# Two-way gated DeltaNet scan on one core: the block inverses of two neighbouring latent tiles in one eight-head group, decays worked in the loaded tile, one ring of six for a step's loads

## The chip, the cores and the metric

The kernel runs on one core of a Trainium2 chip. The metric is the device time of one execution in microseconds. Before the change three runs gave 2559.43, 2563.19 and 2557.81 us, a median of 2559.43.

## What is computed

One step of a diffusion backbone with one layer: 128 context rows and 2048 latent rows of width 1024. Adaptive RMSNorm, one input projection, then two groups of heads side by side (a bidirectional gated DeltaNet with 4 heads of 128, and a gMLP), one output projection, a gated residual, and a squared-ReLU MLP with its own residual. The part that the change touches is the DeltaNet in chunks of 128 rows:

```
a_mat = where(strict, (k_beta @ k.T) * decay, 0)          # per chunk and head, 128 x 128
sol   = triangular_solve(a_mat + I, [v*beta, k_beta*exp(g)])
qk    = (q @ k.T) * decay
v_new = u - w @ S;   o = qd @ S + qk @ v_new;   S = S*exp(g_last) + kd.T @ v_new
```

`decay[i, j]` is exp(g_i - g_j) for j up to i and 0 beyond, where g is the running sum of the log gates. The chunks of one direction form a chain through the state S. The backward direction is the same on the flipped sequence. The inverse of (a_mat + I) does not depend on S, so it can be made ahead of the chain.

## The kernel before

**Stages.** The trace shows three. Up to about 440 us the input projection, the convolution and the first projections of the gMLP run. From about 440 to 1205 us runs the scan. From 1205 us to the end run the MLP's products with weights and activations split into a high and a low part (three matmuls each, L241, L242 and L243, of 128 x 512).

**Units.** A tile is 128 rows of one sequence: one context tile and 16 latent ones. A unit is one tile in one direction, all four heads. There are 34: units 0 to 16 go forward, 17 to 33 backward, and 0 and 17 are the context tile. The turn from forward to backward lies at about 868 to 892 us. While the units run, TensorE fills the room between their steps with large projections, the "fills": gate, u and v projections of the gMLP in the forward half, the output projection in the backward half.

**The preparation of a unit** (called prep, 15 steps) makes T, the inverse times beta/2:

1. Decay E (L1054 Abs of g_j - g_i per head, L1055 Exp, both on ScalarE). The rows of g lie in tile gb, loaded as one row repeated on all partitions (L990). GpSimd then makes a strict triangle Es (L1059) and an inclusive one E (L1061).
2. KK, the loaded k k^T (L1031), is multiplied by beta and Es (L1071, VectorE, one instruction a head), GpSimd sets its diagonal to one (L1075), ScalarE casts it to f16 as AH (L1080), and VectorE cuts X, the 2 x 2 diagonal blocks, from it (L1081).
3. Y is X transposed: a matmul with the identity (L1089) and a ScalarE cast (L1091). VectorE makes AL = KK - AH (L1092).
4. For each block size s of 2, 4, 8, 16 and 32 two steps. The **A step**: four 128 x 64 matmuls AH by Y (L1109), then VectorE multiplies the product in PSUM by a mask into P (L1113). The **B step**: four matmuls X by P (L1122) and four P by X (L1124), then ScalarE casts the results into Y (L1125) and X (L1126). So each A step needs the Y cast of the level below, and each B step needs the P of its own A step.
5. Level 64 in two steps (L1141 to L1153), one refinement R (L1159 to L1162, VectorE), and T (L1171, ScalarE, one instruction a head).

After level 2's B step VectorE also multiplies the loaded QK = q k^T by E (L1129).

**The scan of a unit** is four steps of four 128 x 128 f32 matmuls each (helper L1026): S,kT into vt (L1183), and S,qT into o; vt,T into vs and vn (L1196, L1198, the latter on ScalarE); vs,kt into the new S (L1212); vn,QK into the output o (L1226 to L1233).

**Loads.** All DMAs are issued by SyncE in the order of the program. An issue waits until its destination is free, and what stands behind it waits too. gb, kt, kT, vt and qT have two buffers each, QK has three, and E, Es and KK share a ring of six. A QK load waits for the vn,QK matmuls of three units before.

**Order.** Each step is emitted at an event time (`at`, in units of a tile; WINDOWS holds starts and ends), a fill's first matmul is held behind the latest chain or prep matmul (LAG2 and LAG3 say which), and a scheduler with its own timeline then fixes the order on each engine. `calm` holds an operation behind the newest level operations. On the chip every engine takes its instructions in that written order.

Of the kernel before, what the change touches and what calls it, by code (L numbers as in the profile page):

```python
# [8 lines left out]
F32 = mybir.dt.float32  # L9
# [8 lines left out]
P = 128  # L18
# [3 lines left out]
NT = 17  # L22
# [8 lines left out]
def interleave(*lists):  # L31
# [5 lines left out]
    for _, _, _, s in sorted(order, key=lambda e: e[:3]):  # L37
# [4 lines left out]
BA = 3  # L42
BX = 3
BT = 1
NS = 4
NE = 6
AHEAD_OF = {0: (("v", 7), ("u", 0)), 1: (("u", 1), ("u", 2)), 2: (("u", 3), ("u", 4))}
# [12 lines left out]
WINDOWS = [2.46, 0.03, -0.51, 1.06, -1.61, 18.16, 17.58, 18.3,  # L60
           2.63, -0.06, -0.18, 1.0, 1.36, 1.64, 1.66, 2.66, 3.17, 3.71]
# [3 lines left out]
def hybrid_step(  # L65
# [82 lines left out]
    def bc4(ap):  # L148
        return ap.unsqueeze(1).to_broadcast([P, 4, P])
# [810 lines left out]
    with ExitStack() as ph:  # L960
# [17 lines left out]
        def f16(tag, bufs=1):  # L978
            return pp.tile([P, 4, P], F16, tag=tag, name=tag, bufs=bufs)
# [4 lines left out]
        def s32(name):  # L984
            return pp.tile([P, 4, P], F32, tag="e", name=name, bufs=NE)

        def load_rows(src, t, d):
            gb = q32("gb", 2)
            rows = src[t * 8 + d * 4 : t * 8 + d * 4 + 4, :].rearrange("a b -> (a b)").unsqueeze(0)
            load(out=gb.rearrange("p h d -> p (h d)"), in_=rows.to_broadcast([P, 512]))  # L990
            return gb

        identq = f16("identq")
        V.tensor_copy(identq, bc4(ident16))
# [21 lines left out]
        def unit(t, d):  # L1016
# [7 lines left out]
            def quad(p, lhs, rhs):  # L1024
                for h in range(H):
                    T.matmul(p[:, h, :], lhs[:, h, :], rhs[:, h, :], start=True, stop=True)  # L1026

            def prep_loads():
                u["gb"] = load_rows(g_d, t, d)
                u["KK"] = s32("KK")  # L1030
                load(out=u["KK"], in_=kk_d[t])  # L1031

            def qk_load():
                u["QK"] = q32("QK", 3)
                load(out=u["QK"], in_=qk_d[t])

            def scan_loads():
                for nm, src in (("kt", kt_d), ("kT", kT_d), ("vt", vt_d), ("qT", qT_d)):
                    u[nm] = q32(nm, 2)
                    if nm in ("kT", "qT"):  # L1040
                        load(out=u[nm], in_=src[t])
                    else:
                        load(out=u[nm], in_=src[t * P : (t + 1) * P, :].rearrange("p (h d) -> p h d", h=H))

            prep = []
            scan = []

            @prep.append
            def _():
                e = s32("E")  # L1050

                def decay():
                    for h in range(H):
                        A.activation(e[:, h, :], u["gb"][:, h, :], AF.Abs, scale=-1.0, bias=col(gcol, h))  # L1054
                    A.activation(e, e, AF.Exp, scale=-1.0)  # L1055

                calm(decay, 2)
                es = s32("Es")
                G.affine_select(out=es, in_=e, pattern=[[0, 4], [-sg, P]], compare_op=ALU.is_gt, fill=0.0,  # L1059
                                base=0, channel_multiplier=sg)  # L1060
                G.affine_select(out=e, in_=e, pattern=[[0, 4], [sg, P]], compare_op=ALU.is_ge, fill=0.0,  # L1061
                                base=0, channel_multiplier=-sg)
                u["Es"], u["E"] = es, e

            @prep.append
            def _():
                a = u["KK"]

                def decayed():
                    for h in range(H):  # L1070
                        V.scalar_tensor_tensor(out=a[:, h, :], in0=a[:, h, :], scalar=col(beta, h),  # L1071
                                               in1=u["Es"][:, h, :], op0=ALU.mult, op1=ALU.mult)

                calm(decayed, 1 if d else 2)
                G.affine_select(out=a, in_=a, pattern=[[0, 4], [1, P]], compare_op=ALU.not_equal, fill=1.0,  # L1075
                                base=0, channel_multiplier=-1)
                u["AH"], u["AL"], u["X"] = f16("AH", BA), f16("AL", BA), f16("X", BX)

                def parts():
                    A.copy(u["AH"], a)  # L1080
                    V.tensor_tensor(out=u["X"], in0=u["AH"], in1=bc4(bd2), op=ALU.mult)  # L1081

                calm(parts)

            @prep.append
            def _():
                p = pd()
                for h in range(H):
                    T.matmul(p[:, h, :], u["X"][:, h, :], ident16, start=True, stop=True)  # L1089
                u["Y"] = f16("Y", BX)  # L1090
                A.copy(u["Y"], p)  # L1091
                V.tensor_tensor(out=u["AL"], in0=u["KK"], in1=u["AH"], op=ALU.subtract)  # L1092

            def level(s):

                def half(ap, i):
                    return ap.rearrange("p h (a t b) -> p h a t b", t=2, b=s)[:, :, :, i, :]

                def packed(p, i):
                    return p[:, :, i * 64 : i * 64 + 64].rearrange("p h (a b) -> p h a b", b=s)  # L1100

                yi = 1 - d

                @prep.append
                def _():
                    p = pd()
                    pp, y = packed(p, 0), half(u["Y"], yi)
                    for h in range(H):
                        T.matmul(pp[:, h], u["AH"][:, h, :], y[:, h], start=True, stop=True)  # L1109
                    u["P"] = pms[s]  # L1110
                    if t == 0:
                        V.tensor_copy(pms[s], identq)
                    V.tensor_tensor(out=half(u["P"], yi), in0=pp, in1=half(bc4(sm[s]), yi), op=ALU.mult)  # L1113
                    level_done(s)

                @prep.append
                def _():
                    p = pd()
                    py, px = packed(p, 0), packed(p, 1)
                    y, x, pm = half(u["Y"], yi), half(u["X"], 1 - yi), half(u["P"], yi)  # L1120
                    for h in range(H):
                        T.matmul(py[:, h], u["X"][:, h, :], pm[:, h], start=True, stop=True)  # L1122
                    for h in range(H):
                        T.matmul(px[:, h], u["P"][:, h, :], x[:, h], start=True, stop=True)  # L1124
                    A.copy(y, py)  # L1125
                    A.copy(x, px)  # L1126
                    level_done(s)
                    if s == 2:
                        V.tensor_tensor(out=u["QK"], in0=u["QK"], in1=u["E"], op=ALU.mult)  # L1129

            for s in (2, 4, 8, 16, 32):
                level(s)

            lo, hi = slice(0, 64), slice(64, P)
            ra, rb = (lo, hi) if d == 0 else (hi, lo)

            @prep.append
            def _():
                p = pd()
                for h in range(H):  # L1140
                    T.matmul(p[:, h, 0:64], u["AH"][:, h, :], u["Y"][:, h, rb], start=True, stop=True)  # L1141
                A.activation(pms[64][ra, :, rb], p[ra, :, 0:64], AF.Copy, scale=-1.0)

            @prep.append
            def _():
                p = pd()
                for h in range(H):
                    T.matmul(p[:, h, 0:64], u["X"][:, h, :], pms[64][:, h, rb], start=True, stop=True)
                for h in range(H):
                    T.matmul(p[:, h, 64:P], pms[64][:, h, :], u["X"][:, h, ra], start=True, stop=True)  # L1150
                V.tensor_copy(u["Y"][ra, :, rb], p[ra, :, 0:64])
                level_done(64)
                A.copy(u["X"][rb, :, ra], p[rb, :, 64:P])  # L1153

            @prep.append
            def _():
                p = pd()
                for h in range(H):
                    T.matmul(p[:, h, :], u["AH"][:, h, :], u["Y"][:, h, :], start=True, stop=False)  # L1159
                    T.matmul(p[:, h, :], u["AL"][:, h, :], u["Y"][:, h, :], start=False, stop=True)  # L1160
                u["R"] = f16("R", 1)
                V.scalar_tensor_tensor(out=u["R"], in0=p, scalar=-1.0, in1=bc4(two16), op0=ALU.mult,  # L1162
                                       op1=ALU.add)

            @prep.append
            def _():
                p = pd()
                quad(p, u["X"], u["R"])
                u["T"] = q32("T", BT)
                for h in range(H):  # L1170
                    A.activation(u["T"][:, h, :], p[:, h, :], AF.Copy, scale=col(hbeta, h))  # L1171
# [940 lines left out]
```

## Time and profile before

| what | us |
|---|---|
| runs: median (lowest to highest) | 2559.43 (2557.81 to 2563.19) |
| span of the profiled execution, first to last instruction | 2557.2 |
| forward units, 440 to 868 | 428.0, of it TensorE busy 426.5 |
| turn, 868 to 892 | 24.0, of it TensorE busy 21.0 |
| backward units, 892 to 1205 | 313.0, of it TensorE busy 308.2 |
| VectorE, ScalarE, GpSimd busy in the whole span | 1826.9, 1259.7, 227.5 |

The profiled execution's span lies 2.2 us below the median of the runs; what surrounds the span is no part of it.

A row of a timeline gives the start, the duration, the engine, the line, the operation with out<-in, and in brackets the idle time of the engine just before it and what ended it. A group gives count, total busy time, mean duration in ns, then the engine's idle time before these instructions and what ended most of it. PE is TensorE, PEld its weight loads, DVE VectorE, ACT ScalarE, POOL GpSimd, SPq the DMA queue of SyncE.

### The profile page before, as it was taken

The numbers are of one execution on the slowest core, as the hardware profiler recorded it, in microseconds if no ns is written. First come the engines' busy times: TensorE is split into PE (matmuls) and PEld (weight loads), VectorE is DVE, ScalarE is ACT, GpSimd is POOL, SyncE is SP. The second block draws the span as 40 slices with busy tenths as digits, with TensorE's granted clock in tenths as the row PEclk, the third lists the DMA queues.
The fourth block names the chain that finished last, engine by engine and source line by source line (L and its number), as shares of the span: only waits on it lengthen the run. The fifth ranks groups of instructions, "written<-read, shape, count | busy, mean of one in ns | idle before, by whom it ended". The sixth has DMA issues, their size and how long they took to land.

```text
span 2557.2 us, 44375 instructions
## 1 busy us (share of the span) xinstructions
PE 2532.0 (99%) x15268; PEld 2133.5 (83%) x15268; DVE 1826.9 (71%) x3790; ACT 1259.7 (49%) x3119; POOL 227.5 (9%) x448
## 2 busy tenths in 40 slices
PE   9999999999999999999999999999999999999998
PEld 5899999788888788888888888888887888888887
DVE  5867746777677878886677877777665557684875
ACT  4755555555555767763455544444442433243442
POOL 3112212111111111110000000000000000000000
PEclk9999999999999999999999999999999999999999
DMA  8977747754445657885877789655489979786673
GB/s 286 303 227 208 211 117 230 246 165 154 146 157 166 217 186 247 270 294 181 300 221 232 245 289 338 198 174 176 143 268 365 336 269 329 249 263 208 223 261 112
DMA packets 503912, 588.66 MB, mean 230 GB/s; under 512 B 36148, under 2 KB 298588, under 8 KB 500102
## 3 DMA queue, kind: packets, MB, share of 16 engines
q1 hardware_dynamic: 503686, 585.82, 70.6%
q8 instruction: 120, 1.97, 0.3%
q14 instruction: 106, 0.87, 0.1%
HBM read 406.01 MB, written 179.67 MB: 229 GB/s over the span
## 4 chain that ended last, share of the span: by engine, by line
PE 86%; DMA 7%; DVE 3%; ACT 2%; issue 1%; SPq 0%; POOL 0%; POOLq 0%; DVEq 0%; ACTq 0%
PE f L241 16%; PE f L243 16%; PE f L242 16%; PE pj L241 7%; PE pj L242 7%; PE pj L243 7%; PE pd L1026 5%; PE pm L241 2%; PE pm L243 2%; PE pm L242 2%; DMA r<-in_w_ff_dram 1%; PE pt L625 1%; DMA raw<-in_w_mod_dram 1%; PE pt L584 1%; PE pd L1109 1%
## 5 line engine op out<-in xcount | busy, mean ns | idle before, releaser
L241 PE MATMUL f<-hop,zH 128*128 128x512 f32 (+1 forms) x976 | 376.4, 386 | 1.8 <-ACT zH L1572 1.8
L243 PE MATMUL f<-hop,zL 128*128 128x512 f32 (+1 forms) x976 | 376.4, 386 | 0.0
L242 PE MATMUL f<-hop,zH 128*128 128x512 f32 (+1 forms) x976 | 376.2, 386 | 0.0
L241 PE MATMUL f<-hop,wH 128*128 128x512 f32 x896 | 349.6, 391 | 1.4 <-ACT p L1645 0.8
L242 PE MATMUL f<-hop,wH 128*128 128x512 f32 x896 | 348.7, 389 | 0.0
L243 PE MATMUL f<-hop,wL 128*128 128x512 f32 x896 | 347.5, 389 | 0.0
L1572 ACT CAST zH<-zraw 128x512 fp32r<-128x512 f32 x240 | 147.0, 620 | 307.8 <-DVE zraw L1566 84.6
L241 PEld LDWEIGHTS f<-hop,zH 128*128 128x128 f32 x976 | 183.3, 188 | 39.8 <-ACT zH L1572 3.3
L243 PEld LDWEIGHTS f<-hop,zL 128*128 128x128 f32 x976 | 183.3, 188 | 38.4 <-DVE zL L1566 1.7
L242 PEld LDWEIGHTS f<-hop,zH 128*128 128x128 f32 x976 | 183.3, 188 | 37.0 <-issue 0.2
L1566 DVE TENSOR_TENSOR zL<-zraw,zH 128x512 fp32r<-128x512 f32 x240 | 162.9, 687 | 61.7 <-ACT zH L1572 49.9
L241 PEld LDWEIGHTS f<-hop,wH 128*128 128x128 f32 x896 | 168.2, 188 | 37.1 <-ACT p L1645 2.0
L243 PEld LDWEIGHTS f<-hop,wL 128*128 128x128 f32 x896 | 168.2, 188 | 35.4
L242 PEld LDWEIGHTS f<-hop,wH 128*128 128x128 f32 x896 | 168.2, 188 | 34.5
L241 PE MATMUL pj<-kH,wH 128*128 128x386 f32 (+2 forms) x568 | 190.5, 338 | 1.7 <-ACT junk L601 1.1
L243 PE MATMUL pj<-kH,wL 128*128 128x386 f32 (+2 forms) x568 | 189.7, 335 | 0.0
L242 PE MATMUL pj<-kL,wH 128*128 128x386 f32 (+2 forms) x568 | 189.4, 335 | 0.0
L184 POOL TENSOR_TENSOR r<-rsq,nhalf 128x1 f32<-128x1 f32 (+1 forms) x37 | 23.8, 643 | 1381.3 <-DVE rsq L183 1381.3
L571 DVE SCALAR_TENSOR_TENSOR cv<-pj,vec,cv 128x384 f32<-128x384 f32 (+2 forms) x164 | 87.0, 539 | 53.6 <-ACT cv L568 52.2
L1572 ACT CAST wH<-s 128x512 fp32r<-128x512 f32 x96 | 59.4, 621 | 124.5 <-DVE s L1566 112.4
L202 DVE TENSOR_TENSOR wL<-raw,wH 128x512 fp32r<-128x512 f32 x120 | 81.4, 684 | 42.2 <-ACT wH L201 38.1
L241 PEld LDWEIGHTS pj<-kH,wH 128*128 128x128 f32 x568 | 107.0, 189 | 5.3 <-issue 2.6
(423 smaller groups left out, 5782.6 us busy)
## 6 DMA issues: line engine op xcount, KB each, us to landing
zraw<-z_d SPq DMA_DIRECT2D x212, 256.0 KB
raw<-in_w_ff_dram SPq DMA_DIRECT2D x192, 256.0 KB
hop<-hop_d SPq DMA_DIRECT2D x28, 1024.0 KB
z_d<-c SPq DMA_DIRECT2D x96, 256.0 KB
zraw<-s_d SPq DMA_DIRECT2D x96, 256.0 KB
raw<-in_w_mod_dram SPq DMA_DIRECT2D x80, 256.0 KB
r<-in_w_ff_dram SPq DMA_DIRECT2D x80, 256.0 KB
s_d<-s SPq DMA_DIRECT2D x64, 256.0 KB
```

The source lines that it names most:

```text
L184: G.tensor_tensor(out=out, in0=t[:np_, :n], in1=nhalf[:np_, :n], op=ALU.pow)
L202: V.tensor_tensor(out=lo, in0=raw, in1=f32(h), op=ALU.subtract)
L241: T.matmul(ps, lh, rh, start=first and i == 0, stop=False, skip_group_check=more)
L242: T.matmul(ps, lh, rl, start=False, stop=False, skip_group_check=more)
L243: T.matmul(ps, ll, rh, start=False, stop=last and i == n - 1, skip_group_check=more)
L571: V.scalar_tensor_tensor(out=cv[:, o : o + m], in0=ps[:, s + sh : s + sh + m], scalar=convw[:, w, j : j + 1], in1=cv[:, o : o + m], op0=AL ...
L584: T.transpose(pq[:, i * P : (i + 1) * P], u["x2"][:, i * P : (i + 1) * P], ident)
L625: T.matmul(ps[:, i * P : (i + 1) * P], kTt[:, i * P : (i + 1) * P], rhs[:, i * P : (i + 1) * P], start=True, stop=True)
L1026: T.matmul(p[:, h, :], lhs[:, h, :], rhs[:, h, :], start=True, stop=True)
L1109: T.matmul(pp[:, h], u["AH"][:, h, :], y[:, h], start=True, stop=True)
L1566: V.tensor_tensor(out=out, in0=a, in1=b, op=op)
L1572: A.copy(h, src)
```

## The change

Two neighbouring units of a direction now form a **group** (units 0 and 17 stay alone; 1-2, 3-4 and so on, 18 groups in all). A group's prep has the same 15 steps, each on eight heads in tiles of 128 x 8 x 128:

- One VectorE or ScalarE instruction does for both tiles what two did: P (now L1202), the casts Y and X (L1213, L1214), AH, X, AL, the level-64 pieces and Exp. Still one a tile or a head: Abs (L1138), KK (L1149), the casts of the first Y (L1174), R and T. The matmuls are the same ones in the same number.
- g is loaded straight into E (L1125), which has one buffer; Es is gone. KK (L1126) has one buffer. Both triangles are selected on KK and on E in place. Abs and Exp work in place on E. E is read last when VectorE multiplies the second tile's QK by it (L1130), which is emitted after the B step of level 16; for the first tile it stays after level 2.
- kT, vt, qT and kt of a step (L1030, L1032) share one ring of six buffers.
- AH, X and Y have two buffers, T two. A group's prep is spread over 2.2 (forward) or 2.3 (backward) tile times, where a unit's was spread over 2.46 or 2.63; the group is emitted at its first unit's time. The loads of QK come at i - 2.6 or i - 2 where they came at i - 3, the loads of E and KK at i - 2.7.

```
 def f16(tag, bufs=1):
-    return pp.tile([P, 4, P], F16, tag=tag, name=tag, bufs=bufs)
+    return pp.tile([P, 2 * H, P], F16, tag=tag, name=tag, bufs=bufs)
 def s32(name):
-    return pp.tile([P, 4, P], F32, tag="e", name=name, bufs=NE)
+    return pp.tile([P, 2 * H, P], F32, tag=name, name=name, bufs=1)
...
+        def prep_loads():
+            g["E"], g["KK"] = s32("E")[:, :nh], s32("KK")[:, :nh]
+            for i, u in enumerate(us):
...
+                load(out=g["E"][:, heads(i)].rearrange("p h d -> p (h d)"), in_=rows.to_broadcast([P, 512]))
+                load(out=g["KK"][:, heads(i)], in_=kk_d[t])
+        def decayed_qk(i):
+            u = us[i]
+            V.tensor_tensor(out=u["QK"], in0=u["QK"], in1=g["E"][:, heads(i)], op=ALU.mult)
...
+                for h in range(nh):
+                    T.matmul(pp[:, h], g["AH"][:, h, :], y[:, h], start=True, stop=True)
...
+                V.tensor_tensor(out=half(pm, yi), in0=pp, in1=half(bch(sm[s], nh), yi), op=ALU.mult)
...
+                A.copy(y, py)
+                A.copy(x, px)
+                level_done(s)
+                if s == 2:
+                    decayed_qk(0)
+                elif s == 16 and n == 2:
+                    decayed_qk(1)
...
-WINDOWS = [2.46, 0.03, -0.51, 1.06, -1.61, 18.16, 17.58, 18.3,
-           2.63, -0.06, -0.18, 1.0, 1.36, 1.64, 1.66, 2.66, 3.17, 3.71]
+WINDOWS = [2.2, 0.03, -0.51, 1.06, -1.61, 18.16, 17.58, 18.3,
+           2.3, -0.06, -0.18, 1.0, 1.36, 1.64, 1.66, 2.66, 3.17, 3.71]
```

**Where the order moves.** Three places, in the forward half. The first is TensorE just ahead of a B step of level 2 before the change. Rows are of unit 5: P_5790 is the P of level 2, P_5793 that of level 16 of unit 4, L241 to L243 are fills:

```order
L1124 MATMUL pd<-X,P_5793 128x64
L1124 LDWEIGHTS P_5793
L1124 MATMUL pd<-X,P_5793 128x64
L1026 MATMUL pd<-vt,T 128x128 x4
L241 MATMUL pm<-wH,hH 128x512
L242 MATMUL pm<-wL,hH 128x512
L243 MATMUL pm<-wH,hL 128x512
L241 MATMUL pm<-wH,hH 128x512
L242 MATMUL pm<-wL,hH 128x512
L243 MATMUL pm<-wH,hL 128x512
L1122 LDWEIGHTS X
L1122 MATMUL pd<-P_5790,X 128x64
```

Its A step stands further up, ahead of the other unit's level. After the change, the same place of the group of units 7 and 8, with P_5788 as the P of level 2:

```order
L241 MATMUL pj<-wL,hH 128x512
L242 MATMUL pj<-wH,hL 128x512
L1199 LDWEIGHTS AH
L1199 MATMUL pd<-Y,AH 128x64
L1199 LDWEIGHTS AH
L1199 MATMUL pd<-Y,AH 128x64
L1199 LDWEIGHTS AH
L1199 MATMUL pd<-Y,AH 128x64
L1199 LDWEIGHTS AH
L1199 MATMUL pd<-Y,AH 128x64
L1210 LDWEIGHTS X
L1210 MATMUL pd<-P_5788,X 128x64
```

The second four matmuls of the A step (the first four stand six fills higher) are followed at once by the B step that reads P_5788. The second place is SyncE's queue. Before, the loads of g went into gb and waited for ScalarE (its Abs on that buffer, two units earlier):

```order
L1035 DMA QK_8428<-qk_d_68 128x512 [waits DMAHW3_49,PE_49]
L1235 DMA of_d_70<-o_8321 128x512 [waits DMAHW4_49,DVE_49]
L1290 DMA gate_d_71<-gw_8749 128x512 [waits DMAHW5_49,DVE_49]
L1043 DMA vt_9049<-vt_d_66 128x512 [waits DMAHW6_49,PE_49]
L990 DMA gb_9374<-g_d_69 128x512 [waits DMAHW7_49,Activation_49]
L1031 DMA KK_9055<-kk_d_67 128x512 [waits DMAHW0_49,Pool_49]
L1043 DMA kt_9045<-kt_d_65 128x512 [waits DMAHW1_49,PE_49]
```

After, they go into E and wait for VectorE, whose last reader of E is the multiplication of QK_8885, loaded two rows higher behind a wait for TensorE:

```order
L1301 DMA hL_8955<-hL_d_62 128x512 [waits DMAHW4_49,PE_49]
L1024 DMA QK_8885<-qk_d_68 128x512 [waits DMAHW5_49,PE_49]
L1098 DMA of_d_70<-o_8504 128x512 [waits DMAHW6_49,DVE_49,Activation_49]
L1125 DMA E_8975<-g_d_69 128x512 [waits DMAHW7_49,DVE_49]
L1125 DMA E_8975<-g_d_69 128x512 [waits DMAHW0_49]
```

The third place is ScalarE. Before, the Abs of a unit stand between a Y and X cast of one level and the next without a wait of their own:

```order
L1125 CAST Y<-pd 128x128x2 [waits PE_49,Activation_49]
L1126 CAST X<-pd 128x128x2
L1054 ACTIVATE E<-gb,gcol 128x128 x4
L1198 COPY vn<-pd 128x512 [waits DVE_49]
L1055 ACTIVATE E<-E 128x512 [waits Activation_49]
L1257 ACTIVATE gw<-pm 128x512 [waits DMAHW5_49,PE_49]
L1125 CAST Y<-pd 128x8x32 [waits PE_49]
```

After, the Abs of a group wait for the two DMAs into E_8975, and seven of the eight stand ahead of the Y cast of level 16 of the group before:

```order
L1214 CAST X_8618<-pd_8852 128x64x8 [waits PE_49,Activation_49]
L1138 ACTIVATE E_8975<-E_8975,gcol_191 128x128 [waits DMAHW7_49,DVE_49]
L1138 ACTIVATE E_8975<-E_8975,gcol_191 128x128 x3
L1138 ACTIVATE E_8975<-E_8975,gcol_191 128x128 [waits DMAHW0_49]
L1138 ACTIVATE E_8975<-E_8975,gcol_191 128x128
L1061 COPY vn_8917<-pd_8910 128x512 [waits DVE_49]
L1138 ACTIVATE E_8975<-E_8975,gcol_191 128x128
L1213 CAST Y_8648<-pd_8922 128x32x16 [waits PE_49,Activation_49]
```

Neighbouring Abs that belong to one tile are a head each. TensorE's order before 440 us is the same in both kernels.

More of the change, by code (lines that the diff above doesn't have):

```diff
@@ L41 @@
 MOD_STEPS = (1, 1, 0, 0, 0, 1, 0, 2, 0, 1, 1, 2)
-BA = 3
-BX = 3
-BT = 1
+BA = 2
 NS = 4
-NE = 6
-AHEAD_OF = {0: (("v", 7), ("u", 0)), 1: (("u", 1), ("u", 2)), 2: (("u", 3), ("u", 4))}
+NQ = 3
+NL = 6
+AHEAD_OF = {0: (("v", 7), ("u", 0)), 1: (("u", 1), ("u", 2), ("u", 3), ("u", 4))}
 LATER = {0: (("u", 5),), 1: (("u", 6),)}
@@ L984, in s32, with bch, quad @@
         def s32(name):
-            return pp.tile([P, 4, P], F32, tag="e", name=name, bufs=NE)
[L987 to L994, printed above, removed]
+            return pp.tile([P, 2 * H, P], F32, tag=name, name=name, bufs=1)
+        def bch(ap, n):
+            return ap.unsqueeze(1).to_broadcast([P, n, P])
+        def quad(p, lhs, rhs):
+            for h in range(H):
+                T.matmul(p[:, h, :], lhs[:, h, :], rhs[:, h, :], start=True, stop=True)
         pms = {s: f16(f"P{s}") for s in (2, 4, 8, 16, 32, 64)}
@@ L1022, in col @@
                 return tab[:, t, d * 4 + h : d * 4 + h + 1]
[L1024 to L1031, printed above, removed]
             def qk_load():
-                u["QK"] = q32("QK", 3)
+                u["QK"] = q32("QK", NQ)
                 load(out=u["QK"], in_=qk_d[t])
             def scan_loads():
-                for nm, src in (("kt", kt_d), ("kT", kT_d), ("vt", vt_d), ("qT", qT_d)):
-                    u[nm] = q32(nm, 2)
+                for nm, src in (("kT", kT_d), ("vt", vt_d), ("qT", qT_d), ("kt", kt_d)):
+                    u[nm] = q32("ld", NL)
                     if nm in ("kT", "qT"):
@@ L1043, in scan_loads @@
                         load(out=u[nm], in_=src[t * P : (t + 1) * P, :].rearrange("p (h d) -> p h d", h=H))
-            prep = []
             scan = []
[L1048 to L1171, printed above, removed]
             def scaled(out, p, table):
@@ L1196, in _ @@
                 V.tensor_tensor(out=u["vs"], in0=p, in1=cols, op=ALU.mult)
-                u["vn"] = q32("vn", BT)
+                u["vn"] = q32("vn", 1)
                 A.copy(u["vn"], p)
@@ L1242, in hybrid_step @@
         units = [unit(t, 0) for t in range(NT)] + [unit(t, 1) for t in [0] + list(range(NT - 1, 0, -1))]
+        groups = {i: group(units[i : i + (1 if i % NT == 0 else 2)])
+                  for o in (0, NT) for i in [o] + list(range(o + 1, o + NT, 2))}
         def f2_steps(t):
```

144 lines of the change are left out of this document (131 added, 13 removed).

## The prediction

> **What bounds the kernel now.** I read the page first, then the busy time by stage, then who TensorE waits for in the three parts of the scan. From the page:
>
> ```profile
> span 2557.2 us, 44375 instructions
> PE 2532.0 (99%) x15268; PEld 2133.5 (83%) x15268; DVE 1826.9 (71%) x3790; ACT 1259.7 (49%) x3119; POOL 227.5 (9%) x448
> PEclk9999999999999999999999999999999999999999
> ```
>
> TensorE is busy for 99% of the span at full clock in every slice; no other engine comes near. By stage (length, then busy time of PE, PEld, DVE, ACT and POOL, clock, DMA share, GB/s):
>
> ```profile
> 440.00:868.00 428.00, 426.48 (x3640) 353.74 (x3638) 306.63 (x865) 235.70 (x636) 59.90 (x80) 1.00 0.56 180
> 868.00:892.00 24.00, 20.96 (x220) 18.00 (x220) 21.91 (x58) 15.62 (x47) 2.92 (x4) 1.00 0.57 190
> 892.00:1205.00 313.00, 308.24 (x2702) 257.58 (x2701) 252.00 (x630) 211.10 (x663) 49.03 (x59) 1.00 0.72 241
> 1205.00:2557.20 1352.20, 1342.22 (x6033) 1109.15 (x6031) 950.35 (x1558) 550.07 (x1045) 18.61 (x27) 1.00 0.75 246
> ```
>
> In the scan, 440 to 1205, TensorE idles for 428.0 - 426.5 = 1.5 us forward, 3.0 at the turn and 4.8 backward. That is all that a faster VectorE or ScalarE can give back: 9.3 us. The waits of TensorE in the three parts:
>
> ```profile
> PE pm L243 <- DMA hL<-hL_d: 1.0, 1, 1.0
> PE pd L1109 <- ACT Y L1125: 0.4, 1, 0.4
> ```
>
> ```profile
> PE pd L1109 <- ACT Y L1125: 1.8, 3, 0.8
> PE pd L1159 <- DVE Y L1151: 0.7, 1, 0.7
> PE pm L1384 <- DVE ug L1264: 0.5, 1, 0.5
> ```
>
> ```profile
> PE pj L241 <- DVE tmp L1407: 1.7, 3, 0.8
> PE pd L1141 <- ACT Y L1125: 1.3, 2, 0.9
> PE pm L241 <- DVE tmp L1407: 1.2, 3, 0.5
> ```
>
> Forward, nothing of the preparation holds TensorE up but once, for 0.4 us. So the question is not how much the merged instructions save, but whether every latency still lies under TensorE's work.
>
> **Merging the small operations.** The operations in question, with count, busy time and mean:
>
> ```profile
> L1113 DVE TENSOR_TENSOR P<-pd,sm 128x256 f16<-128x256 f32 x170 | 68.6, 417 | 34.4 <-PE pd L1109 33.8
> L1125 ACT CAST Y<-pd 128x256 f16<-128x256 f32 x170 | 66.1, 389 | 42.8 <-PE pd L1124 42.4
> L1126 ACT CAST X<-pd 128x256 f16<-128x256 f32 x170 | 68.4, 402 | 0.0
> L1162 DVE SCALAR_TENSOR_TENSOR R<-pd,two 128x512 f16<-128x512 f32 x34 | 23.3, 685 | 8.1 <-PE pd L1160 8.1
> L1091 ACT CAST Y<-pd 128x512 f16<-128x512 f32 x34 | 20.1, 591 | 24.2 <-PE pd L1089 24.2
> L1054 ACT ACTIVATE E<-gb,gcol 128x128 f32<-128x128 f32 x136 | 44.7, 430 | 0.0
> L1129 DVE TENSOR_TENSOR QK<-QK,E 128x512 f32<-128x512 f32 x34 | 23.5, 691 | 38.8 <-DMA QK<-qk_d 38.1 <-POOL KK L1075 0.8
> ```
>
> A P on 256 elements takes 417 ns, a VectorE operation from PSUM on 512 takes 685 (R). Two into one saves 2 x 417 - 685 = 149 ns; 80 mergers of P save 12 us of VectorE. A cast on 256 takes 0.39 to 0.40, on 512 0.59 us, so a merger saves 0.2 and 160 of them 32 us of ScalarE. On TensorE's path this is worth only the waits above. Of the turn's 3.0 I credit 2.0 (its Y casts). Of the backward 4.2 I credit 2.8: 2.9 wait for tmp L1407, queued on VectorE, and 1.3 for Y casts. TensorE's matmuls are the same; in the order, fills start behind a cluster of small matmuls 325 times instead of 330. The first such fill takes about 0.08 longer (0.31 against 0.23, below), so 0.4 us. **Gains: 5.2 us.**
>
> But the merged step has a longer latency, and fewer preps run side by side to cover it.
>
> **The B step of level 2.** An A step, its P and the fills:
>
> ```profile
> 593.80 0.28 PE L1109 MATMUL pd<-Y,AH 128*128 128x64 f16 x4
> 594.11 0.48 PE L241 MATMUL pj<-wH,hH 128*128 128x512 f32 x1
> 594.27 0.42 DVE L1113 TENSOR_TENSOR P<-pd,sm 128x256 f16<-128x256 f32 x1
> 594.42 0.39 PE L242 MATMUL pj<-wL,hH 128*128 128x512 f32 x1
> 594.66 0.40 PE L243 MATMUL pj<-wH,hL 128*128 128x512 f32 x1
> 595.35 0.40 PE L243 MATMUL pj<-wH,hL 128*128 128x512 f32 x1
> ```
>
> VectorE starts 0.19 us after the matmuls' end (594.27 - 594.08). A P of eight heads then takes 0.685, so its reader can start about 0.9 us after the A step ends. A fill takes (595.35 - 594.42)/4 = 0.232. Before, six fills and more stood there, 1.4 us. In the new order of the group of units 7 and 8 the B step stands directly behind the second half of the A step: no cover, and TensorE waits 0.9 us. I counted the matmuls at this place in every forward group: six have none, one has fills for 0.3. **6 x 0.92 + 0.6 = 6.1 us.** The bounds are 4.5 (P starts 0.2 earlier on a matmul end that is modelled) and 8 (P found behind another VectorE operation of 0.4 to 0.7 twice in three).
>
> **Backward.** Counted in the same way, B steps of levels 2 and 32 have 0.1 to 1.0 us of cover against 0.92, which makes 2.7 + 1.4; the transposes of the output steps stand closer to their casts, another 2 or so. **6 us**, bounds 2 and 9.
>
> **E with one buffer.** This is the largest term. The loads of g into E wait for VectorE's multiplication of the second tile's QK in the group before. That waits for the QK load, which waits for the vn,QK matmuls of three units earlier. Before:
>
> ```profile
> 635.49 1.05 PE L1026 MATMUL pd<-vn,QK 128*128 128x128 f32 x8
> 636.58 0.32 SPq L1035 DMA_DIRECT2D QK<-qk_d  x1
> 636.30 0.47 PE L241 MATMUL pj<-wH,hH 128*128 128x512 f32 x1
> 638.41 0.29 PE L1109 MATMUL pd<-Y,AH 128*128 128x64 f16 x4
> 638.54 0.28 PE L1122 MATMUL pd<-P,X 128*128 128x64 f16 x4
> 639.15 0.69 DVE L1129 TENSOR_TENSOR QK<-QK,E 128x512 f32<-128x512 f32 x1 [0.50 <-DMA QK<-qk_d]
> 639.76 0.42 DVE L1113 TENSOR_TENSOR P<-pd,sm 128x256 f16<-128x256 f32 x1
> ```
>
> TensorE can go on at 636.30; the QK load is issued at 636.58, and VectorE can use it at 639.15, 2.57 after its issue. All 34 units make VectorE idle 38.1 us for this load (L1129). Today nothing but QK hangs on that, and gb's load waits only for an Abs of two units earlier, so L1054 idles 0.0. After the change a second load of 2.57 (QK's, of the same 256 KB) follows in series: 2.85 to the start of the multiplication, 0.69 for it, 0.1 for two wake-ups, 2.57 for E: 6.2 us from the vn,QK step to the first Abs. In the order of ScalarE, 2 to 8 of these Abs (0.43 each), sometimes a copy or two (0.6 each), stand ahead of the Y cast of level 16, for which the next A step of TensorE waits (0.63 with its wake-up).
>
> On the other side stands what TensorE has to do between vn,QK and that A step, counted in the order and priced from the rows: 128 x 64 matmuls 0.03 (638.54 - 638.41, four), a fill 0.232, the four f32 matmuls of a scan step 0.81 (636.30 - 635.49), 0.08 for each change to fills. For the E of units 11 and 12: 40 x 0.03 + 21 x 0.232 + 2 x 0.81 + 4 x 0.08 = 8.0 us of work. The chain is 6.2 + 7 x 0.43 + 0.6 + 0.63 = 10.4. TensorE waits 2.4 us. The seven forward places:
>
> | E of units | work of TensorE | Abs and copies ahead | chain | wait |
> |---|---|---|---|---|
> | 5, 6 | 8.6 | 8, 2 | 11.5 | 2.9 |
> | 9, 10 | 7.9 | 8, 2 | 11.5 | 3.6 |
> | 11, 12 | 8.0 | 7, 1 | 10.4 | 2.4 |
> | 13, 14 | 7.2 | 2, 0 | 7.7 | 0.5 |
> | 15, 16 | 8.0 | 7, 0 | 9.8 | 1.8 |
> | 17 | 7.2 | 4, 0 | 8.6 | 1.4 |
> | 20, 21 | 8.1 | 4, 0 | 8.6 | 0.5 |
>
> The E of units 7 and 8 has 12.7 us of work and costs nothing. **13 us in all.** Both loads 0.5 us faster: 7; both 0.5 slower: 20. The row at 639.76 bears on this: its A step ended at 638.70, yet P started only behind the waiting QK multiplication. [...] If ScalarE could take the Y cast past a waiting Abs, this term would be nothing, the first rival below. [...]
>
> **The rest at nothing.** The ring of six: a step's four loads find the buffers of matmuls long past, in the order always the preceding step's; under that cover a late load would cost what the SPq wait lasts. Selecting on KK and E in place lengthens the start of a group's prep, which has over 8 us of fills ahead of its first matmul. The larger GpSimd pieces lie on the same cover.
>
> **Sum.** 13 + 6.1 + 6 - 5.2 = 19.9 us on a span of 2557.2, 2577.1; with the 2.2 by which the runs' median stands above the span, **2579 us**. About 0.2%, 5 us, is what a measurement of this kernel can tell from no change.
>
> **Rivals.**
>
> *No blocked casts (15%).* Loads land sooner in the less loaded forward half, or a cast passes the Abs. Then 6.1 + 6 - 5.2 = 7, 2566 us. For it: the chain has to be under 7.2 to 8.6 us, and places with few Abs miss that by 0.5. Against it: three places miss by over 2 us.
>
> *Faster through the fills (12%).* Fills in the MLP, where fewer small operations run:
>
> ```profile
> 1699.91 0.39 PE L241 MATMUL f<-hop,wH 128*128 128x512 f32 x1
> 1701.95 0.39 PE L241 MATMUL f<-hop,wH 128*128 128x512 f32 x1
> ```
>
> Nine fills in 2.04 us are 0.227 each, against 0.232 in the scan. If VectorE's and ScalarE's many accesses cause this, fewer instructions return some of it. At 3 ns on the 1900 fills of the scan (counted in the order) that is 5.7 us, and if all 7.2 us of turn and backward waits go, and no cast is blocked nor a backward cover short: 6.1 - 5.7 - 7.2 - 0.4 = -7.2, 2552 us. It decides from 1.8 ns a fill upward (6.1 - 3.5 - 7.2 - 0.4 = -5). Against it: VectorE is 70% busy in the MLP too (950 of 1352).
>
> *E late backward too (13%).* The backward loads are slower:
>
> ```profile
> 1019.15 0.74 SPq L1035 DMA_DIRECT2D QK<-qk_d  x1
> 1026.32 0.69 DVE L1129 TENSOR_TENSOR QK<-QK,E 128x512 f32<-128x512 f32 x1 [2.43 <-DMA QK<-qk_d]
> ```
>
> 7.17 us instead of 2.57. Backward groups have 12.4 to 13.1 us of work over a chain of 8.6 with forward loads. Two loads at 5.2 make 13.8, a wait of 1 us; two at 7.17 make 17.8, nearly 5. Over six groups 6 to 30 us; at 15, 2594 us.
>
> *No effect (7%).* TensorE's instructions are the same and it is 99% busy: 2559 us. Against it: the 99% holds only while latencies are covered, and the covers are what the order changes.
>
> **How the numbers follow.** My forecast has 53%. Faster: the second rival, and one in a hundred beyond it, 0.13. Same: no effect, and the low end of the first, 0.11. Slower: 0.76. The forecast's own bounds (E 7 to 20, level 2 4.5 to 8, backward 2 to 9) added as independent give 2579 -8 +9. The range reaches down to 2554, to let in the no-effect case, and up to 2602, which holds three quarters of the late backward case.
>
> **What would show it.** After: waits of TensorE at the A step of level 32 for the Y cast (L1213), 0.5 to 3.6 us, at seven forward places, ScalarE idle ahead of Abs (L1138) for the DMA of E, some 15 us; waits at L1210 for P (L1202) of 0.9, six forward; TensorE's forward idle near 20 us instead of 1.5; ScalarE some 40 us less busy. It is wrong if the forward stage is no longer than 430 us, if Abs doesn't idle, or if TensorE waits but for other lines.

## The result and the profile after

The changed kernel takes 2634.34 us (median of four runs, 2629.15 to 2639.35) against 2560.74 for the kernel before on the same chips: ratio 1.0291, 95% interval 1.0276 to 1.0305. That is 74 us slower, where 20 were forecast. The page of the changed kernel, span and busy times:

```profile
span 2630.0 us, 43993 instructions
PE 2548.1 (97%) x15268; PEld 2143.2 (81%) x15268; DVE 1814.4 (69%) x3661; ACT 1240.5 (47%) x2895; POOL 216.4 (8%) x400
```

TensorE issues the same 15268 instructions. VectorE and ScalarE are 12 and 19 us less busy. The span is 73 us longer. To see where, I put the stretches between the same points of the work beside each other: from the scan's first prep matmul (the transposing of X, L1089, now L1173) to the vn,QK step of unit 16, from there to that of unit 33, and the rest. Before:

```profile
450.00:852.00 402.00, 400.48 (x3466) 333.14 (x3465) 284.37 (x800) 217.72 (x594) 53.76 (x72) 1.00 0.54 174
852.00:1200.00 348.00, 340.19 (x3021) 283.65 (x3021) 285.81 (x726) 237.71 (x733) 56.01 (x68) 1.00 0.71 236
```

After (the columns are those of the stages in the prediction; behind POOL's stands the granted clock):

```profile
451.00:892.00 441.00, 412.76 (x3484) 338.15 (x3483) 276.50 (x733) 209.95 (x479) 47.96 (x45) 0.98 0.48 155
892.00:916.00 24.00, 21.37 (x192) 17.47 (x190) 20.05 (x52) 17.04 (x35) 6.09 (x5) 0.93 0.58 175
916.00:1273.00 357.00, 322.56 (x2815) 270.31 (x2813) 261.07 (x615) 209.65 (x589) 43.74 (x42) 1.00 0.68 224
1273.00:2630.00 1357.00, 1346.92 (x6059) 1113.32 (x6057) 952.53 (x1565) 551.26 (x1053) 18.25 (x27) 1.00 0.75 246
```

Forward 402 became 441, turn and backward 348 became 381, and the rest is what it was (2557 - 1200 and 2630 - 1273 are both 1357). So 39 us come from the forward half and 33 from the turn and backward. TensorE's busy time rose too, by 16 us, although its work is the same; a granted clock below one accounts for part of that (below). What TensorE waits for, forward and then from unit 16 on:

```profile
PE pd L1199 <- ACT Y L1213: 13.7, 7, 2.9
PE pd L1210 <- DVE P L1202: 9.3, 11, 2.6
PE pd L1173 <- DVE X L1163: 2.2, 1, 2.2
PE pd L1199 <- ACT Y L1174: 2.1, 1, 2.1
```

```profile
PE pd L1210 <- DVE P L1202: 13.5, 14, 2.0
PE pd L1199 <- ACT Y L1174: 7.0, 7, 1.4
PE pd L1173 <- ACT o L1038: 3.0, 2, 1.6
PE pd L1231 <- ACT Y L1213: 2.7, 3, 1.6
```

**The E chain is there, at the places forecast.** The seven A steps of level 32 that wait for their Y cast, in the trace's order of time (the rows between them left out; the seventh wait of the forward list, 0.87 us at 459.5, is of another level, and the last row here lies in the turn):

```profile
542.10 0.39 PE L1199 MATMUL pd<-Y,AH 128*128 128x64 f16 x8 [2.44 <-ACT Y L1213]
...
637.53 0.59 PE L1199 MATMUL pd<-Y,AH 128*128 128x64 f16 x8 [2.93 <-ACT Y L1213]
...
686.88 0.39 PE L1199 MATMUL pd<-Y,AH 128*128 128x64 f16 x8 [2.50 <-ACT Y L1213]
...
735.09 0.39 PE L1199 MATMUL pd<-Y,AH 128*128 128x64 f16 x8 [0.96 <-ACT Y L1213]
...
781.16 0.39 PE L1199 MATMUL pd<-Y,AH 128*128 128x64 f16 x8 [1.97 <-ACT Y L1213]
...
827.89 0.44 PE L1199 MATMUL pd<-Y,AH 128*128 128x64 f16 x8 [2.02 <-ACT Y L1213]
...
903.40 0.42 PE L1199 MATMUL pd<-Y,AH 128*128 128x64 f16 x5 [2.22 <-ACT Y L1213]
```

They sum to 15.0 us; the prediction's table has 2.9, 3.6, 2.4, 0.5, 1.8, 1.4 and 0.5, together 13.1. The second one link by link:

```profile
629.52 0.69 DVE L1130 TENSOR_TENSOR QK<-QK,E 128x512 f32<-128x512 f32 x1 [2.08 <-DMA QK<-qk_d]
630.24 0.80 SPq L1125 DMA_DIRECT2D E<-g_d  x2
633.57 1.57 ACT L1138 ACTIVATE E<-E,gcol 128x128 f32<-128x128 f32 x5 [2.88 <-DMA E<-g_d]
635.56 0.97 ACT L1138 ACTIVATE E<-E,gcol 128x128 f32<-128x128 f32 x3
636.44 0.56 ACT L1061 COPY vn<-pd 128x512 f32<-128x512 f32 x1
636.90 0.58 ACT L1213 CAST Y<-pd 128x512 f16<-128x512 f32 x1
```

VectorE waits for the QK load, the E load goes out at the end of the multiplication, ScalarE stands before its first Abs for 2.88 us, and the Y cast, whose matmuls had long ended, comes behind eight Abs and two other operations. In the whole span ScalarE idles 46.5 us for this DMA:

```profile
ACT E L1138 <- DMA E<-g_d: 46.5, 15, 6.0
```

**The clock is what I had not counted.** Behind the wait of 2.93 us:

```profile
638.51 0.63 PE L241 MATMUL pj<-wL,hH 128*128 128x512 f32 x1
638.93 0.63 PE L242 MATMUL pj<-wH,hL 128*128 128x512 f32 x1
```

Fills stand 0.43 us apart instead of 0.23. Such stretches follow waits of 2 to 3 us forward, some at once and one after 1.2 us (a wait ending at 686.9, slow fills from 688.1); the wait of 2.44 us that ends at 542.1 and one of 2.14 that ends at 853.2 have none behind them. In ten-us slices the clock falls to between 0.83 and 0.98; over the scan its shortfall adds up to 12 us (one less the clock, times ten, over the ten slices below 1.00), of which a part lies in the waits.

### The profile page after: what moved, and what is told of

Same layout as the page of the kernel before. It is cut to its first block, busy times and chain, and to the rows that moved or that the text cites. A ratio compares the mean times of both kernels' runs of the same rounds, so it can differ in the third digit from the quotient of the medians.

```text
span 2630.0 us, 43993 instructions
## 1 busy us (share of the span) xinstructions
PE 2548.1 (97%) x15268; PEld 2143.2 (81%) x15268; DVE 1814.4 (69%) x3661; ACT 1240.5 (47%) x2895; POOL 216.4 (8%) x400
## 3 DMA queue, kind: packets, MB, share of 16 engines
q8 instruction: 120, 1.97, 0.3%
## 4 chain that ended last, share of the span: by engine, by line
PE 81%; DMA 6%; DVE 5%; ACT 4%; issue 2%; POOL 1%; SPq 0%; POOLq 0%; ACTq 0%; DVEq 0%
PE f L240 16%; PE f L242 16%; PE f L241 16%; PE pj L240 6%; PE pj L242 5%; PE pj L241 5%; PE pd L991 4%; DMA QK<-qk_d 3%; DMA E<-g_d 2%; PE pm L240 1%; PE pm L241 1%; PE pm L242 1%; PE pt L624 1%; ACT E L1138 1%; PE pt L583 1%
## 5 line engine op out<-in xcount | busy, mean ns | idle before, releaser
L241 PE MATMUL f<-hop,zH 128*128 128x512 f32 (+1 forms) x976 | 376.2, 386 | 0.0
L241 PE MATMUL f<-hop,wH 128*128 128x512 f32 x896 | 348.7, 389 | 0.0
L241 PEld LDWEIGHTS f<-hop,zH 128*128 128x128 f32 x976 | 183.3, 188 | 37.2 <-DVE hop L1597 0.2
L241 PEld LDWEIGHTS f<-hop,wH 128*128 128x128 f32 x896 | 168.3, 188 | 34.6
L241 PE MATMUL pj<-kL,wH 128*128 128x386 f32 (+2 forms) x568 | 189.5, 335 | 0.1
```

The costliest lines, as they stand in the source:

```text
L241: T.matmul(ps, lh, rl, start=False, stop=False, skip_group_check=more)
```

## Experiments

Theory 1: the loss comes from one chain, the late QK load, the QK multiplication that holds the single E buffer, E's reload, Abs, and what stands behind Abs on ScalarE and behind the multiplication on VectorE, with the low clock as its consequence. Theory 2, its rival: what is lost is cover, because about one eight-head prep runs at a time (2.2 tile times for two tiles) where some 2.5 four-head preps ran side by side. Both can hold in part. Each kernel was timed in the same job as the kernel before, and its ratio is to that.

One thing limits all of these runs: the scheduler orders anew for every kernel. Matched by names and shapes in the traces, some 600 of TensorE's 15268 matmuls stand at another place in the run with four QK buffers than in the changed kernel, as many in the run with three E tiles, some 1000 in the one with P in two, and about 20 in the one with idle matmuls. So a difference in time is that of the edit together with its order, and what an edit did has to be read from the waits as well.

The first four runs take the change apart. **Four QK buffers**:

```
-NQ = 3
-NL = 6
+NQ = 4
+NL = 5
```

> The changed kernel with a fourth buffer for QK (and five instead of six in the ring of a step's loads, to make room). QK's load then waits for the vn,QK step of four units before, one tile time earlier; the order of TensorE keeps its places, level 2's B steps still stand directly behind their A steps. Theory 1 (the chain QK load, QK multiplication, E load, Abs, Y cast is the largest cost, and the half clock follows its long waits): the forward waits for the Y cast (14.8 us) and the low clock (about 8) go, and the five backward waits of 2 us for P, which stand behind a waiting QK multiplication, go too: some 30 us, 2604. Theory 2 (what is lost is cover, because one eight-head prep runs where two four-head ones ran side by side): at most the two largest waits shrink, 2625 to 2634.

Measured: 2592.81 us, ratio 1.0136 (1.0106 to 1.0165), so over half of the loss is gone, 11 us more than theory 1 gave. Waits of TensorE, then ScalarE and VectorE for the two loads:

```profile
PE pd L1210 <- DVE P L1202: 16.6, 22, 1.3
PE pd L1199 <- ACT Y L1174: 7.9, 7, 2.2
```

```profile
ACT E L1138 <- DMA E<-g_d: 6.1, 3, 3.0
```

```profile
DVE QK L1130 <- DMA QK<-qk_d: 15.7, 9, 4.0
```

The wait for the Y cast of a level has left the head of the list, ScalarE's wait for E fell from 46.5 to 6.1 us. Forward (452.2 to 868.7) takes 416.5 us, backward (to 1233.6) 364.9, against 441 and 381. So the late QK load was at the root of the chain on both engines. The operands of the matmuls in the two traces tell the level of each B step: the waits for P at level 16 from the turn on, 8.9 us in the changed kernel, are gone. Those at level 2 forward (8.0 us, now 6.0) and at levels 2 and 32 from the turn on (4.6 us, now 9.2) stay, each 1.3 us at most; they fit theory 2.

**E in three four-head tiles** (the loop over heads of Abs and the select follow suit):

```
-                g["E"], g["KK"] = s32("E")[:, :nh], s32("KK")[:, :nh]
+                g["E"], g["KK"] = [q32("E", 3, pp) for _ in us], s32("KK")[:, :nh]
...
-NL = 6
+NL = 5
```

> The changed kernel with E in a ring of three four-head tiles, one Exp and one select a tile (and five in the ring of a step's loads). The next group's first E no longer waits, its second waits for the first tile's QK multiplication after level 2, long before. Theory 1, if the single E buffer is the cause: Abs no longer waits for a DMA (46.5 us of ScalarE idle now), the forward waits for Y go with the low clock, 2634 - 15 - 8 = 2611; the waits of VectorE for QK's load stay. Theory 2: within 8 of 2634.

Measured: 2609.69 us, ratio 1.0201 (1.0163 to 1.0240), within 2 us of theory 1's figure. VectorE keeps its wait for QK, and TensorE its waits for P:

```profile
DVE QK L1130 <- DMA QK<-qk_d: 45.8, 27, 5.7
PE pd L1212 <- DVE P L1204: 26.5, 32, 3.4
```

The waits for the Y cast at level 32 have gone, and the gain lies forward alone: 420 us there, and 382 from the turn on, where the changed kernel has 381. Of the waits for P, 10.2 us stand at level 16 from the turn on. So the single buffer, with the order that came with it, is worth about 25 us, and the late QK load does harm besides, through VectorE's own queue.

**Everything but the groups** (single units as before, E in place, the ring of six):

```
-            gb = q32("gb", 2)
+            gb = s32("E")
...
-                    u[nm] = q32(nm, 2)
+                    u[nm] = q32("ld", 6)
```

> The kernel before with all of the change but the groups: g loaded into E and worked in place, both triangles selected in place, the ring of six for kT, vt, qT and kt; units single, E and KK still from one ring of six. Theory 1 and theory 2 both put the cost elsewhere: 2561 +- 5. If the longer start of a prep (two selects on KK in series) or the ring costs something, 2570 or more.

Measured: 2555.75 us, ratio 0.9984 (0.9973 to 0.9995). With single units the in-place decays and the ring cost nothing; the run is 3 to 4 us below the kernel before. All of the loss belongs to the groups, with the buffers and event times that came with them.

**P as two instructions** in the changed kernel:

```
-                    V.tensor_tensor(out=half(pm, yi), in0=pp, in1=half(bch(sm[s], nh), yi), op=ALU.mult)
+                    for i in range(n):
+                        V.tensor_tensor(out=half(pm, yi)[:, heads(i)], in0=pp[:, heads(i)],
+                                        in1=half(bch(sm[s], H), yi), op=ALU.mult)
```

> The changed kernel with P of the levels 2 to 32 as two VectorE instructions, one a tile, the scheduler then ordering anew. Theory 2 (the merged step's latency without cover): the first half of a B step can start 0.3 us earlier and stands beside other work; the waits for P (24.9 us in all) fall by a third, 2625. Theory 1: the E chain stays, 2634 +- 5.

Measured: 2658.79 us, ratio 1.0393 (1.0363 to 1.0424), a miss for both. TensorE's longest wait in the scan:

```profile
PE pd L1199 <- ACT Y L1215: 35.1, 30, 3.4
```

The scheduler, with other durations, wrote another order, and the Y cast now waits at thirty places instead of eight. It says nothing about P's latency, because the order changed with it.

**Both mends of the loads together**:

> Both mends of the loads together: QK with four buffers and E in a ring of three four-head tiles (room from five buffers in the ring of a step's loads and seven in the fills' input ring). The order of TensorE's steps stays as in the changed kernel, B steps of level 2 directly behind their A steps. If what is left of the loss (33 us in the run with four QK buffers alone) is lost cover, this gains next to nothing over it: 2588 to 2593. If the single E buffer still costs there (Abs still idled 6 us for it), 2583 or less.

Measured: 2611.98 us, ratio 1.0205 (1.0175 to 1.0235): a miss, 19 us above four QK buffers alone. Forward takes the same 416.4 us (451.03 to 867.45). The difference lies in and behind the turn (385 us against 365), about half of it in two slices (columns as in the stages, the clock behind POOL's):

```profile
900.00:910.00 10.00, 5.47 (x41) 4.92 (x41) 8.76 (x35) 6.66 (x20) 1.01 (x1) 0.70 0.56 180
910.00:920.00 10.00, 8.36 (x81) 7.82 (x79) 8.62 (x28) 4.50 (x9) 1.98 (x2) 0.62 0.17 54
```

In the new order VectorE is busy for 8.8 and ScalarE for 6.7 of the ten us from 900, TensorE stands for 4.5, and the clock goes. With E out of the way an order can still lose some 10 us at one place.

**More overlap**: four QK buffers, preps spread over 3.2 and 3.3 tile times, the loads of QK 1.2 and those of E and KK one tile time earlier:

```
-WINDOWS = [2.2, 0.03, -0.51, 1.06, -1.61, 18.16, 17.58, 18.3,
-           2.3, -0.06, -0.18, 1.0, 1.36, 1.64, 1.66, 2.66, 3.17, 3.71]
+WINDOWS = [3.2, 0.03, -0.51, 1.06, -1.61, 18.16, 17.58, 18.3,
+           3.3, -0.06, -0.18, 1.0, 1.36, 1.64, 1.66, 2.66, 3.17, 3.71]
```

> The run with four QK buffers, with the prep of a group spread over 3.2 and 3.3 tile times instead of 2.2 and 2.3 (its loads one tile time earlier), so that two groups' preps overlap by half. In the new order B steps of level 2 and 32 have 1.2 to 3.4 us of TensorE's work between P and reader where they had 0 to 1.6. Theory 2: the waits for P (19.8 us in the four-buffer run) fall under 5 and the time to 2560 to 2572. E has one buffer still: if its reuse then holds Abs back, waits for the Y cast come instead and it stays at 2580 to 2600. Theory 1 alone: 2593.

Measured: 2583.82 us, ratio 1.0095 (1.0066 to 1.0124), in the range given for the case that E's reuse holds Abs back.

```profile
PE pd L1173 <- DVE X L1163: 8.1, 3, 5.9
PE pm L240 <- ACT oH L1415: 7.0, 2, 3.7
PE pd L1210 <- DVE P L1202: 5.4, 6, 1.5
```

```profile
ACT E L1138 <- DMA E<-g_d: 29.4, 14, 3.8
```

The waits for P fell from 16.6 to 5.4 us as theory 2 has it, and the stretch from the turn on from 365 to 356 us. In their place came a late first pair (5.9 us at X) and ScalarE held by Abs again (29.4 us idle), with oH twice behind eight Abs and an Exp.

**The same with E in three tiles** (and seven buffers instead of eight in the fills' input ring) was to take that away:

> As the run before, with E in the ring of three four-head tiles. Both causes are then out of the way: 2552 to 2560, that is the time of the kernel with everything but the groups (2556) less some of the 9 us that TensorE waited in the kernel before. If the merged steps cost something of their own, 2565 or more.

Measured: 2584.70 us, ratio 1.0098 (1.0069 to 1.0128): no gain, and 25 us above the forecast. Its waits for P are 12.0 us again, one of 4.2 at the turn. The order is another one here too, so the run doesn't show whether that or a cost of the merged steps keeps it up.

**The first pair kept at 2.2**, E with one buffer:

> The run with groups spread over 3.2 and 3.3 tile times and four QK buffers, its first pair kept at 2.2, so that the 6.0 us wait for that pair's X at 461 us goes. If that wait is a plain loss of its own: 2578 (5 to 6 less than 2584). If the pairs after it then press later: 2584.

Measured: 2572.72 us, ratio 1.0053 (1.0033 to 1.0074), 11 us less than without, more than the wait's 6 and below both forecasts. At X 3.8 us are left. It is the fastest grouped kernel here, 14 us over the kernel before.

**One prep at a time, single units.** The run with everything but the groups, with its WINDOWS starting at 1.25 instead of 2.46 and 2.63:

> The kernel with everything but the groups (single units, four-head steps, E and KK from the ring of six), with a unit's prep spread over 1.25 tile times instead of 2.46 and 2.63, so that about one prep runs at a time, as in the changed kernel (2.2 tile times for two tiles). No operation is merged. Theory 2 (the cover is lost because fewer preps run side by side, whatever the size of their operations): waits for P and for the Y cast of 0.3 to 1 us appear throughout, 25 us or more, 2580 to 2600. If it is the merged operations' longer latency that costs: 2556 to 2565. The E and QK loads are not in question here.

Measured: 2648.05 us, ratio 1.0348 (1.0327 to 1.0369).

```profile
PE pd L1108 <- ACT Y L1124: 23.1, 41, 1.1
PE pd L1121 <- DVE P L1112: 15.9, 25, 1.9
```

That is 48 us above the upper end of theory 2's forecast. No operation is merged here, VectorE never waits for a QK load and ScalarE only once for E (2.2 us), and yet it loses 92 us against the same kernel with 2.5 preps side by side: 56 us in many short waits, most of the rest in a longer busy time of TensorE at a clock of 1.00, which I can't place. With a tile time of about 21 us a unit then has 1.25 x 21 / 15 = 1.8 us a step, a group in the changed kernel 2.2 x 21 / 15 = 3.1. So one prep at a time costs by itself, without merged operations. A group loses less by it, 33 us over the kernel before with four QK buffers; its steps are also further apart, so the two numbers don't divide the groups' own loss.

**The clock.** 36 matmuls of 56 ns that nobody reads, ahead of eight A steps of level 32, in the changed kernel:

```
+                    if s == 32 and d == 0 and n == 2:
+                        w = pd()
+                        for k in range(36):
+                            T.matmul(w[:, k % H, :], two16, ident16, start=True, stop=True)
```

> The changed kernel with 36 idle f16 matmuls of 128 x 128 (2.0 us, into a PSUM tile that nothing reads) ahead of the A step of level 32 of the eight forward pairs, where TensorE waits for the Y cast. They add 16 us of work of which some 12 fall into waits. If the low clock follows from TensorE standing idle, the granted clock of the forward stage rises from 0.98 to 1.00, the fills spaced 0.43 us vanish there, and the time is 2630 to 2636. If the clock falls for another reason, it stays at 0.98 and the time rises to 2638 or more.

Measured: 2633.45 us, ratio 1.0289 (1.0259 to 1.0319). In the changed kernel the slices around the waits have

```profile
610.00:620.00 10.00, 7.53 (x55) 6.58 (x54) 5.88 (x15) 2.29 (x4) 0.00 (x0) 0.83 0.22 61
630.00:640.00 10.00, 7.07 (x58) 5.73 (x56) 6.29 (x21) 5.95 (x14) 1.01 (x1) 0.85 0.42 131
```

and with the idle matmuls

```profile
610.00:620.00 10.00, 9.22 (x89) 7.43 (x88) 5.50 (x15) 3.31 (x7) 0.00 (x0) 1.00 0.41 128
640.00:650.00 10.00, 9.49 (x73) 8.13 (x73) 4.88 (x14) 4.31 (x7) 3.19 (x3) 0.70 0.25 79
```

16 us more work on TensorE cost no time. In the forward half the clock falls below 1.00 only around 640 us (0.96 and 0.70), at a wait of 3.1 us for P that no idle matmul covers; at 612 us the wait itself is gone. So the low clock went with the standing still here; the stage's mean rose only to 0.99, not to the 1.00 expected, for that one place. What the low clock cost in time this run doesn't say: the shortfall over the scan fell from 12 to 5 us, but the idle matmuls and longer waits for P (14.0 us forward instead of 9.3) came in its place.

**A version that beats both.** Everything but the groups, with a fourth QK buffer:

> The kernel with everything but the groups, with a fourth buffer for QK, whose load is emitted half a tile earlier. VectorE's idle time for that load (37 us) should fall under 10. TensorE waits little for VectorE there: if the queue behind it is what makes the waits for tmp and P at the turn and backward (about 5 us), 2550 to 2554; if not, 2556.

Measured: 2554.25 us, ratio 0.9984 (0.9974 to 0.9993): 4 us (0.2%) below the kernel before and 80 below the changed one. VectorE's wait for the QK load is gone from its list, but the time is that of the run without the fourth buffer: TensorE had not waited for that queue.

## Where the prediction held and where it failed

*Merging, gains of 5.2 us.* Not visible. The casts into Y and X cost ScalarE 33 us less, as worked out, but the waits of TensorE that were to go are replaced by longer ones. The in-place part and the ring, costed at nothing, are free in the kernel with single units.

*B step of level 2, 6.1 us forward.* Right in place and somewhat short: 8.0 us at seven B steps of level 2, and 9.3 at eleven waits with those of levels 4 and 8. Typical is this one, with no fill between:

```profile
566.04 0.29 PE L1199 MATMUL pd<-Y,AH 128*128 128x64 f16 x4
567.12 0.40 PE L1210 MATMUL pd<-P,X 128*128 128x64 f16 x8 [0.78 <-DVE P L1202]
```

At one of these places, 612 us, TensorE waited 2.62 us, because VectorE came to P only behind four other kinds of work (L1332, L1059, L1286, L1287). With four QK buffers the waits of level 2 forward sum to 6.0.

*E with one buffer, 13 us.* Right in the chain and in the seven places: 15.0 us. The sum is in part luck. The reload of E took 3.3 to 4.1 us from its issue to the first Abs where the prediction had 2.57; the Abs follow each other every 0.31 us (five in 1.57) where it had 0.43; and the last place waited 2.22 us where it had 0.5. ScalarE's idle time ahead of Abs, given as some 15 us, came out at 46.5. The rival in which no cast is blocked is out: the Y cast at 636.90 followed the last Abs and a copy, while its matmuls had ended before 634. In the traces of both kernels every engine's operations start, line for line, in the order written (ScalarE's 2827 before, its 2603 after). What the term left out is the clock: TensorE's longest idle in the rows of before was 1.0 us, and I took its clock of 1.00 as given for waits of two to three.

*Backward, 6 us.* This is the step that failed. It counted covers of levels 2 and 32 and of the transposes, and took VectorE and ScalarE as free when needed; the rival weighed only the E chain on ScalarE. Turn and backward lost 33 us, of it 29 in waits. The largest part of the waits for P, 8.9 of 13.5 us, stands at the B step of level 16, which the count left out. It was put at nothing there because the late QK load was followed to E and ScalarE, and not to the P that stands behind the QK multiplication on VectorE, although the prediction's own row at 639.76 shows such a P. The trace has, for example:

```profile
1127.21 0.38 SPq L1024 DMA_DIRECT2D QK<-qk_d  x1
1132.07 0.69 DVE L1130 TENSOR_TENSOR QK<-QK,E 128x512 f32<-128x512 f32 x1 [1.85 <-DMA QK<-qk_d]
1135.56 0.68 DVE L1202 TENSOR_TENSOR P<-pd,sm 128x512 f16<-128x512 f32 x1
1136.30 0.39 PE L1210 MATMUL pd<-P,X 128*128 128x64 f16 x8 [1.84 <-DVE P L1202]
```

The A step ended at 1133.0. VectorE had stood for a QK load that took 4.9 us, and worked off what had gathered before it came to P; four more waits for P of 1.5 to 2.0 us, all of level 16, end in the same way, behind a QK multiplication that waited for its load and operations on the output (L1094 each time). The QK multiplication waited before the change too (21.8 us from the turn on), but TensorE waited for no P in the scan then. Four QK buffers took 16 us of the 33 and every wait at level 16; three E tiles took none of either. Of the 17 left, the run with 3.2 and 3.3 tile times took another 8. A second term that the sum doesn't have is the first A step of a group, directly behind its transposes: it waits for the casts of the first Y (L1174), 7.0 us from the turn on and 2.1 forward, and 7.9 with four QK buffers.

*The time.* 13 + 6 forward stands against 39 measured: waits of about 27 and, by the clock column, up to 9 lost to the low clock, with some 3 more of busy time that the trace doesn't place. From the turn on 6, less gains of 4.8, stands against 33. The forecast's range ended at 2602, since the late-backward rival was priced on one engine alone.

What stays open: how the 33 us left with four QK buffers divide between lost cover, the merged steps' latency and the single E; the runs that were to split it (P in two, both mends together) changed the order as well. The runs don't show a grouped kernel as fast as the single one; a longer spread with three E tiles was not run beyond 3.3 tile times.

## What to carry to other kernels

When TensorE is busy for 99% of the time, count what independent work stands beside each step of a dependent chain: merging two chains into one leaves about half as many side by side, and the fewer, larger operations on the other engines bought nothing back here. When a buffer is cut to one, follow its release through every engine's queue: here a late load of another tile held the release, the reload, and behind it a cast that had nothing to do with either. Follow the late load itself through the queue of the engine that waits for it, too: on VectorE it held P at a level that nobody had counted.

## What the runs showed of the hardware

In the changed kernel TensorE's clock dropped behind some of its waits of 2 to 3 us, in a stream that was otherwise full: fills stood 0.43 us apart instead of 0.23, for one to four us. Length alone didn't decide. Of the nine waits of 1.9 to 3 us up to 910 us in the changed kernel, those of 2.02 (to 827.9), 2.22, 2.23, 2.50, 2.62 and 2.93 have slow fills behind them, those of 1.97, 2.14 and 2.44 (to 542.1) have none; and around 930 us four waits of 0.7 to 1.4 us within some seven us have them too.
